# Hybrid encoder layer on one Trainium2 core: four blocks of the first FFN with one group by sevens, and the preparation, the first quarters and a block's norms in another order

## The chip, the core and the metric

One core of a Trainium2 chip runs one launch of the kernel. The time is the device time of that launch in microseconds, the median of several executions. The engines are named as the profile names them: PE is TensorE (matmuls; PEld its weight loads), DVE is VectorE, ACT is ScalarE, POOL is GpSimd and SP is SyncE, which only issues DMAs. ACT and POOL issue DMAs too.

## The reference

One layer of a streaming encoder, for 256 positions of width 2048, all in float32:

```
x = x + 0.5 * swiglu(rms_norm(x, ffn1_norm), ffn1_w_gate, ffn1_w_up, ffn1_w_down)
h = rms_norm(x, mix_norm);  u, q, k, v = split(h @ w_in)
y_ssm = s5_mixer(u, ...)                 # diagonal complex state space, 64 groups of 16 channels
y_sb  = stick_breaking_attention(rms_norm(q), rms_norm(k), v)      # 8 heads of 128
x = x + concat(rms_norm(y_ssm), rms_norm(y_sb)) @ w_out
x = x + 0.5 * swiglu(rms_norm(x, ffn2_norm), ffn2_w_gate, ffn2_w_up, ffn2_w_down)
x = x + rms_norm((p @ w_ple_proj) * sigmoid(rms_norm(x, ple_norm) @ w_ple_gate))

def swiglu(h, w_gate, w_up, w_down):
    return (silu(h @ w_gate) * (h @ w_up)) @ w_down
```

The hidden width of an FFN is 5632. The S5 mixer needs matrices that depend on the parameters alone (powers of the discretised state matrix, its products with B and C); the kernel computes them itself. This is called the preparation below.

## The kernel before, in words

**Products.** A float32 matrix product is made of three products of float32r parts. `split` (L179) casts a tile to its high part on ScalarE (`whi`, `nhi`; L182) and subtracts that from the tile on VectorE to get the low part (`wlo`, `nlo`; L185). `gemm_half` (L295) then multiplies, for two k tiles of 128 rows, high by high and low by high (L301, 8 matmuls of 512 columns for the two row blocks of 128 positions) and high by low (L308, 4 matmuls). A quarter is four k tiles of one weight matrix, 512 columns wide: one load of 1 MB on SP's queue into one of three `raw` buffers, two splits, 24 matmuls. `gemm_block` (L327) runs the four quarters of a block of 512 output columns.

**The FFN** (`ffn`, L538) runs over 11 blocks of 512 hidden columns, gate and up for each, then the down product. A block is plain, or it is a pair: `Pairs` (L357) takes [gate | up] as one matrix and one or two of its four groups of four k tiles by sevens, that is by seven products in place of eight over 2 x 2 blocks (two row blocks, two halves of k, gate and up). `prepare_left` (L367) forms the sums of the activations, four operations of 128 x 256 and a split (`shi`, `slo`); `fetch` (L390) loads both weight tiles (`dg`, `du`) and forms three sums of weights on VectorE (`t1`, `t2`, `t4`, L415) and one on a DMA that adds (`du<-du`, on GpSimd's queue, L419). `sevens` (L423) makes the products (`product`, L310: 4 matmuls of L318 and 2 of L322) into four accumulators, with additions and subtractions between them on VectorE (L431 to L439). `rest` (L462) runs the remaining groups plainly. In the first FFN blocks 0 to 6 are plain and 7 to 10 take two groups by sevens (`FIRST_PAIRS`, L30). In the second FFN block 0 takes one group and the others two; the final gate product has one group as well.

**What runs beside.** Generators stand in a list `beside`; `step` (L104), called after each half, runs each one on to its next yield. `put_off(n, f)` calls f n steps later. So the loads and transposes of norms, the squares for their means, the sums of the weights and the preparation are interleaved with the matmuls by counting steps. The instructions are then put in order for each engine at build time by a planner with its own costs; `pin` keeps an instruction in program order, and `tc.issue_after` ties instructions behind another on its engine. Each engine works through its own queue in order.

**The preparation** (`s5_prep_steps`, L865) starts after block 0 of the first FFN and goes one yield per step until `EARLY`, at which `finish(prep)` runs what is left. Its last part has four rounds `q`: eight complex products (`cmul`, L948: six VectorE operations each), copies into padded tiles on ScalarE, 16 transposes and 16 small matmuls on TensorE, and stores of the results to scratch in DRAM (`scr`), issued by ScalarE. One of them, `m3`, is placed piece by piece in a tile by 16 ScalarE copies (L1077) and stored whole.

**Around it.** `first_quarters` (L245) loads and splits the first two quarters' weights and activations in pieces; the activations' second quarter comes by ACT's queue. `turn_quarters` (L223) finishes a transpose across 128 partitions by 16 DMAs from a tile `mid`, for hidden blocks into DRAM (`hidden`) on SP's queue, and for the normed activations of some blocks on GpSimd's. `Normed.block` (L483) does this for one quarter of x, with `parted` (the split with the gain, L193 and L195) a number of steps later and `squares` after one step. `project` (L1474) makes the output projection and puts off `n2.block` for the second FFN's norm.

Of the kernel before, what the change touches and what calls it, by code (L numbers as in the profile page):

```python
# [28 lines left out]
EARLY = 6  # L29
FIRST_PAIRS = 7,()  # L30
# [7 lines left out]
def layer_kernel(ctx: ExitStack, tc: tile.TileContext, a: dict, shapes: dict, out: bass.AP):  # L38
# [84 lines left out]
    last_sevens = []  # L123

    @contextmanager
    def behind_sevens():
# [96 lines left out]
    def turn_quarters(out, mid, steps, queue=None):  # L223
# [3 lines left out]
        def g():  # L227
            for _ in range(steps):
                yield
            for i in range(4):  # L230
                for q in range(4):
                    (queue or nc.sync).dma_start(  # L232
                        out[32 * q : 32 * q + 32, :, i], mid[32 * i : 32 * i + 32, q]
                    )
# [10 lines left out]
    def first_quarters(w, xn):  # L245

        rest = com("h")
        raws = [wp.tile([P, 4, NB], F32, tag="raw", name=uid("raw"), bufs=3) for _ in range(2)]
        src = [w[i * NB : (i + 1) * NB, :NB].rearrange("(j p) n -> p j n", p=P) for i in range(2)]
        for j in range(4):  # L250
            nc.sync.dma_start(raws[0][:, j, :], src[0][:, j, :])
# [7 lines left out]
        part = halves("n")  # L259
        parts = [[wp.tile([P, 2, NB], F32R, tag=s, name=uid(s)) for s in ("whi", "wlo")] for _ in range(2)]  # L260
        for j in range(4):
            xj = rest[:, (j - 1) * T : j * T] if j else gains[:, NCOL:]
            xhi, xlo = (u[:, j, :] for u in part)
            whi, wlo = (u[:, j % 2, :] for u in parts[j // 2])
            gain = col(xn.gain, j)
            if j:
                pin(nc.scalar.activation(xhi, xj, AF.Copy, scale=gain))
            else:
                pin(nc.vector.tensor_scalar(xhi, xj, gain, None, op0=ALU.mult))
            pin(nc.scalar.copy(whi, raws[0][:, j, :]))  # L270
            pin(nc.vector.scalar_tensor_tensor(
                out=xlo, in0=xj, scalar=gain, in1=xhi.bitcast(F32), op0=ALU.mult, op1=ALU.subtract
            ))
            pin(nc.vector.tensor_tensor(out=wlo, in0=raws[0][:, j, :], in1=whi.bitcast(F32), op=ALU.subtract))
        xn.parts[0] = part
        xn.parted(1, second.rearrange("p (j s) -> p j s", j=4))
        return [(h, *parts[h]) for h in range(2)], weight_split(raws[1], 4)

    def weight_split(raw, nk, own=None):
        for h in range(nk // 2):  # L280
# [4 lines left out]
            split(hi, lo, raw[:, 2 * h : 2 * h + 2, :])  # L285
            yield h, hi, lo

# [7 lines left out]
    def gemm_half(ps, half, ts, start, stop, cols=slice(0, NB), apart=False, **kw):  # L295
# [3 lines left out]
        for j in range(2):  # L299
# [5 lines left out]
        for j in range(2):  # L305
            for t in ts:
                lh = ahi[:, 2 * h + j, t * P : (t + 1) * P]
                nc.tensor.matmul(ps[t], lhsT=lh, rhs=lo[:, j, cols], start=False, stop=stop and j == 1, **kw)  # L308

    def product(ps, a, src, start):  # L310

        (ahi, alo), hi, lo = a, *(wp.tile([P, 2, NB], F32R, tag=s, name=uid(s)) for s in ("whi", "wlo"))
        marks = split(hi, lo, src)

# [12 lines left out]
    def gemm_block(act, w, n0, nkt, first=(), but=None):  # L327

        ps = [acc(), acc()]
        for k0 in range(0, nkt, 4):  # L330
            part = act(k0 // 4)
            quarter = first[k0 // 4] if k0 // 4 < len(first) else weight_halves(w, k0, min(4, nkt - k0), n0)
            for half in list(quarter):
# [4 lines left out]
                step(but if k0 + 4 >= nkt else None)  # L338
# [18 lines left out]
    class Pairs:  # L357
# [5 lines left out]
        def __init__(self, xn, buf):  # L363
            self.xn, self.buf = xn, buf
            self.left, self.right, self.sums = [], {}, {}

        def prepare_left(self, tag="h"):  # L367
# [4 lines left out]
            pin(nc.vector.tensor_tensor(out=full, in0=part[0].bitcast(F32), in1=part[1].bitcast(F32), op=ALU.add))  # L372
# [4 lines left out]
            a11, a12, a21, a22 = (quarter(full, t, k) for t in range(2) for k in range(2))  # L377
            for o, x, y, op in (
                (a22, a21, a22, ALU.subtract), (a21, a11, a21, ALU.subtract), (a11, a22, a11, ALU.subtract),
                (a12, a12, a11, ALU.add),  # L380
# [1312 lines left out]
```

## Time and profile before

| | us |
|---|---|
| median of 3 runs | 1853.39 (1853.13 to 1853.56) |
| the profiled execution | 1853.61 |
| its span | 1851.8 |

| stage, us from the span's start | what runs |
|---|---|
| 0 to 49 | block 0 of the first FFN |
| 49 to 273 | blocks 1 to 5, with the preparation |
| 273 to 317 | block 6 |
| 317 to 482 | blocks 7 to 10, two groups by sevens |
| 482 to 730 | down product |
| 730 to 1047 | mixer, attention, output projection |
| 1047 to 1510 | second FFN, gate and up |
| 1510 to 1852 | down product, the per-layer embedding |

The edges of the stages are read from the activations and gated products of the blocks and are rough by a few us. A row of an engine's timeline gives the start, the duration, the engine, the line, the operation, the tile written and the tiles read, and a count where neighbours of one kind are merged; in brackets stands how long the engine was idle before, and what ended that. Rows of busy time by stage give, for each engine, its busy us and in brackets its number of instructions. A duration of a matmul overlaps with the next ones; its pace is read from start to start.

### The profile page before, as it was taken

The numbers are of one execution on the slowest core, as the hardware profiler recorded it, in microseconds if no ns is written. First come the engines' busy times: TensorE is split into PE (matmuls) and PEld (weight loads), VectorE is DVE, ScalarE is ACT, GpSimd is POOL, SyncE is SP. The second block draws the span as 40 slices with busy tenths as digits, with TensorE's granted clock in tenths as the row PEclk, the third lists the DMA queues.
The fourth block names the chain that finished last, engine by engine and source line by source line (L and its number), as shares of the span: only waits on it lengthen the run. The fifth ranks groups of instructions, "written<-read, shape, count | busy, mean of one in ns | idle before, by whom it ended". The sixth has DMA issues, their size and how long they took to land.

```text
span 1851.8 us, 24382 instructions
## 1 busy us (share of the span) xinstructions
PE 1841.6 (99%) x8884; PEld 1517.1 (82%) x8884; DVE 1501.2 (81%) x1984; ACT 1109.7 (60%) x1354; POOL 108.1 (6%) x174
## 2 busy tenths in 40 slices
PE   9999999999999999999999999999999999999998
PEld 7888878888888888888898788888888888888886
DVE  8895767999777997686556999999889977799865
ACT  7446665566555666455784666556566655566654
POOL 0010000000000002010012510000000000000200
PEclk9999999999999999999999999999999999999999
DMA  9787878676888758675647667878777688875843
GB/s 322 255 273 232 290 257 284 205 227 218 286 262 279 235 192 300 231 259 182 205 137 269 214 203 246 269 237 265 222 244 227 219 289 265 273 237 193 279 156 140
DMA packets 272729, 443.49 MB, mean 239 GB/s; under 512 B 18784, under 2 KB 87776, under 8 KB 272480
## 3 DMA queue, kind: packets, MB, share of 16 engines
q1 hardware_dynamic: 252448, 408.01, 65.1%
q0 software_dynamic: 7392, 18.88, 4.9%
q10 hardware_dynamic: 12768, 15.04, 2.3%
q8 instruction: 69, 1.13, 0.3%
q14 instruction: 52, 0.43, 0.1%
HBM read 393.64 MB, written 26.21 MB: 227 GB/s over the span
## 4 chain that ended last, share of the span: by engine, by line
PE 96%; DMA 2%; DVE 1%; POOL 1%; ACT 0%; issue 0%; SPq 0%; DVEq 0%; POOLq 0%
PE acc L301 47%; PE acc L308 24%; PE acc L318 12%; PE acc L322 6%; PE aux L318 2%; PE aux L322 1%; DMA h<-mid 1%; POOL h L232 1%; DVE wlo L185 0%; PE aux L1134 0%; PE acc L1413 0%; PE acc L1408 0%; PE acc L1404 0%; PE aux L1046 0%; DMA raw<-in_ffn_w_gate 0%
## 5 line engine op out<-in xcount | busy, mean ns | idle before, releaser
L182 ACT CAST whi<-raw 128x1024 fp32r<-128x1024 f32 x506 | 526.0, 1052 | 415.3 <-PE acc L301 290.5
L185 DVE TENSOR_TENSOR wlo<-raw,whi 128x1024 fp32r<-128x1024 f32 x506 | 608.7, 1223 | 201.4 <-ACT whi L182 200.5
L301 PE MATMUL acc<-whi,nhi 128*128 128x512 f32 x1424 | 558.0, 392 | 0.9 <-ACT whi L182 0.4
L301 PE MATMUL acc<-whi,nlo 128*128 128x512 f32 x1424 | 554.3, 389 | 0.0
L308 PE MATMUL acc<-wlo,nhi 128*128 128x512 f32 x1424 | 382.3, 389 | 0.4 <-DVE wlo L185 0.4
L301 PEld LDWEIGHTS acc<-whi,nhi 128*128 128x128 f32 x1424 | 267.1, 188 | 59.1 <-issue 1.6
L308 PEld LDWEIGHTS acc<-wlo,nhi 128*128 128x128 f32 x1424 | 267.2, 188 | 56.6 <-DVE wlo L185 0.8
L301 PEld LDWEIGHTS acc<-whi,nlo 128*128 128x128 f32 x1424 | 267.4, 188 | 54.6
L301 PE MATMUL acc<-whi,hhi 128*128 128x512 f32 x560 | 219.2, 391 | 0.1
L301 PE MATMUL acc<-whi,hlo 128*128 128x512 f32 x560 | 218.3, 390 | 0.0
L182 ACT CAST whi<-t 128x1024 fp32r<-128x1024 f32 x119 | 125.1, 1051 | 108.5 <-PE acc L301 62.9
L185 DVE TENSOR_TENSOR wlo<-t,whi 128x1024 fp32r<-128x1024 f32 x119 | 141.8, 1220 | 32.1 <-ACT whi L182 31.9
L308 PE MATMUL acc<-wlo,hhi 128*128 128x512 f32 x560 | 149.8, 389 | 0.3 <-DVE wlo L185 0.3
L301 PEld LDWEIGHTS acc<-whi,hhi 128*128 128x128 f32 x560 | 105.1, 188 | 24.4 <-ACT whi L182 1.1
L301 PEld LDWEIGHTS acc<-whi,hlo 128*128 128x128 f32 x560 | 105.1, 188 | 22.5
L308 PEld LDWEIGHTS acc<-wlo,hhi 128*128 128x128 f32 x560 | 105.0, 188 | 22.5 <-DVE wlo L185 0.7
L318 PE MATMUL acc<-whi,shi 128*128 128x512 f32 x240 | 95.5, 398 | 0.0
L318 PE MATMUL acc<-whi,slo 128*128 128x512 f32 x240 | 94.3, 393 | 0.0
L182 ACT CAST whi<-dg 128x1024 fp32r<-128x1024 f32 x60 | 63.0, 1051 | 37.6 <-PE acc L301 23.8
L232 POOL DMA_DIRECT2D h<-mid x96 | 51.0, 542 | 582.1 <-DVE mid L218 538.6
L185 DVE TENSOR_TENSOR wlo<-dg,whi 128x1024 fp32r<-128x1024 f32 x60 | 72.4, 1210 | 9.2 <-ACT whi L182 8.7
L322 PE MATMUL acc<-wlo,shi 128*128 128x512 f32 x240 | 75.5, 396 | 0.0
(336 smaller groups left out, 2197.5 us busy)
## 6 DMA issues: line engine op xcount, KB each, us to landing
raw<-in_ffn_w_down SPq DMA_DIRECT2D x68, 1024.0 KB, 6.5
raw<-in_ffn_w_up SPq DMA_DIRECT2D x59, 1024.0 KB, 7.8
raw<-in_ffn_w_gate SPq DMA_DIRECT2D x57, 1024.0 KB, 7.1
raw<-in_w_in SPq DMA_DIRECT2D x32, 1024.0 KB, 5.6
dg<-in_ffn_w_gate SPq DMA_DIRECT2D x29, 1024.0 KB, 7.0
du<-in_ffn_w_up SPq DMA_DIRECT2D x29, 1024.0 KB, 8.7
hf<-hidden SPq DMA_DIRECT2D x44, 512.0 KB, 5.4
raw<-in_w_out SPq DMA_DIRECT2D x16, 1024.0 KB, 5.5
```

Source lines behind the costliest of these rows:

```text
L182: copy = nc.scalar.copy(hi, src)
L185: rest = nc.vector.tensor_tensor(out=lo, in0=src, in1=hi.bitcast(F32), op=ALU.subtract)
L232: (queue or nc.sync).dma_start(out[32 * q : 32 * q + 32, :, i], mid[32 * i : 32 * i + 32, q])
L301: nc.tensor.matmul(ps[t], lhsT=u[:, 2 * h + j, t * P : (t + 1) * P], rhs=hi[:, j, cols], start=t in starts and j == 0 and u is ahi, stop=F ...
L308: nc.tensor.matmul(ps[t], lhsT=lh, rhs=lo[:, j, cols], start=False, stop=stop and j == 1, **kw)
L318: nc.tensor.matmul(ps, lhsT=l[:, j], rhs=hi[:, j], start=start and i + j == 0, stop=False, skip_group_check=True)
L322: nc.tensor.matmul(ps, lhsT=ahi[:, j], rhs=lo[:, j], start=False, stop=j == 1, skip_group_check=True)
```

## The change

- `FIRST_PAIRS` becomes 4,(4,5,6,7): blocks 4 to 7 of the first FFN take one group by sevens, 8 to 10 two. `EARLY` becomes 7.
- The preparation's rounds yield after each complex product; a round's outputs (transposes, small matmuls, stores) run as a generator of their own beside the next round's products. All stores go to GpSimd's queue, in program order. `m3` is no longer placed in a tile: zeros are written to its scratch (`cleared`), and 16 small DMAs write its pieces.
- `behind` ties the preparation, `prepare_left` and the pinned sums of weights behind the last split made; `prepare_left` becomes a generator of three steps. With `weave`, one of the two steps of a quarter comes between its two splits.
- The hidden stores of blocks 0 to 5 go to GpSimd's queue, in program order, four steps earlier.
- `first_quarters` brings the second quarter's activations by SP's queue in two halves, each ahead of its weights, and splits in the order of the halves; within the first quarter the low products of a k tile follow its high products (`gemm_half` with `apart`).
- `n2.block`: other counts of steps for the split and the squares of each of the four blocks, and block 3 begins four steps later.

```diff
-EARLY = 6
-FIRST_PAIRS = 7,()
+EARLY = 7
+FIRST_PAIRS = 4,(4,5,6,7)
...
+    def behind(splits):
         with ExitStack() as held:
-            for ins in last_sevens:
+            for ins in splits:
                 held.enter_context(tc.issue_after(ins))
             yield
...
     def first_quarters(w, xn):
-        rest = com("h")
+        rest, second = com("h"), com("h")
...
-        second = xn.laid(1)
+        for j in range(4):
+            nc.sync.dma_start(raws[0][:, j, :], src[0][:, j, :])
         for j in range(0, 4, 2):
+            nc.sync.dma_start(
+                second[:, j * T : (j + 2) * T], a["turned"][:, NCOL + (4 + j) * T : NCOL + (6 + j) * T]
+            )
             nc.sync.dma_start(raws[1][:, j : j + 2, :], src[1][:, j : j + 2, :])
...
+        for h, whi, wlo in quarters[1]:
+            sl = slice(2 * h, 2 * h + 2)
+            for low in (*activations(1, (2 * h, 2 * h + 1), x1), weights(whi, wlo, raws[1][:, sl, :])):
+                low()
+        return quarters
...
-            split(hi, lo, raw[:, 2 * h : 2 * h + 2, :])
+            last_split[:] = split(hi, lo, raw[:, 2 * h : 2 * h + 2, :])
             yield h, hi, lo
+
+    def woven(quarter, but, weave):
+        if not weave:
+            yield from list(quarter)
+            return
+        first = next(quarter)
+        step(but)
+        second = next(quarter)
+        yield first
+        yield second
...
+        for part, j in ((high, 0), (low, 0), (high, 1), (low, 1)) if apart else ((high, 0), (high, 1), (low, 0), (low, 1)):
+            part(j)
...
-                gemm_half(ps, (part, half), range(TT), k == 0, k + 2 == nkt, apart=bool(first) and k == 0)
+                gemm_half(ps, (part, half), range(TT), k == 0, k + 2 == nkt, apart=bool(first) and k < 4)
...
-                    with behind_sevens():
-                        ins = nc.vector.tensor_tensor(out=o, in0=x, in1=y, op=ALU.add)
-                    if pinned:
-                        pin(ins)
+                    with behind(last_split if pinned else last_sevens):
+                        nc.vector.tensor_tensor(out=o, in0=x, in1=y, op=ALU.add)
...
-                turn_quarters(hf.rearrange("p (t i f b) -> p t i f b", t=TT, i=4, f=n_pair), mids[pair], 8)
+                turn_quarters(
+                    hf.rearrange("p (t i f b) -> p t i f b", t=TT, i=4, f=n_pair), mids[pair], 4 if bg and f < early else 8,
+                    *((nc.gpsimd, pin) if f < early and bg else ()),
+                )
...
-                if len(pairs.left) < n_groups(f + 1):
-                    with behind_sevens():
-                        pairs.prepare_left("sg")
...
+            if f + 1 < NF and len(pairs.left) < n_groups(f + 1):
+                pairs.prepare_left("sg")
...
+        def outputs(q):
...
-                m1 = get(sub, "m1")
+                m1 = get(sub, "m1", bufs=2)
                 nc.scalar.copy(m1, ps)
-                nc.scalar.dma_start(scr[n][q], m1)
+                pin(nc.gpsimd.dma_start(scr[n][q], m1))
...
+            for r in range(4):
+                for sidx in range(SL):
+                    pin(nc.gpsimd.dma_start(
+                        m3[32 * sidx : 32 * sidx + 32, :, r, 32 * sidx :],
+                        rows[32 * r : 32 * r + 32, :, : P - 32 * sidx],
+                    ))
+                yield
+            if q + 1 < NQ:
+                pin(cleared(q + 1))
             yield
...
-            put_off(0, n2.block, n, (1, 9 if n else 6), nc.gpsimd)
+            put_off(0 if n < ND - 1 else 4, n2.block, n, ((1, 6, 3), (1, 9, 3), (1, 12, 3), (1, 6, 4))[n], nc.gpsimd)
```

More of the change, by code (lines that the diff above doesn't have):

```diff
@@ L221, in turn_blocks, with turn_quarters @@
         )
-    def turn_quarters(out, mid, steps, queue=None):
+    def turn_quarters(out, mid, steps, queue=None, held=lambda ins: ins):
         def g():
@@ L261, in first_quarters @@
-        for j in range(4):
[L262 to L274, printed above, removed]
@@ L275, in first_quarters, with activations @@
-        xn.parts[0] = part
-        xn.parted(1, second.rearrange("p (j s) -> p j s", j=4))
-        return [(h, *parts[h]) for h in range(2)], weight_split(raws[1], 4)
+        parts = [halves("n") for _ in range(2)]
+        xn.parts.update(enumerate(parts))
+        quarters = [
+            [(h, *(wp.tile([P, 2, NB], F32R, tag=s, name=uid(s)) for s in ("whi", "wlo"))) for h in range(2)]
+            for _ in range(2)
+        ]
+        def activations(i, js, src):
+            for j in js:
+                xhi, gain = parts[i][0][:, j, :], col(xn.gain, 4 * i + j)
+                if i + j:
+                    pin(nc.scalar.activation(xhi, src[j], AF.Copy, scale=gain))
+                else:
+                    pin(nc.vector.tensor_scalar(xhi, src[j], gain, None, op0=ALU.mult))
+            return [
+                lambda j=j: pin(nc.vector.scalar_tensor_tensor(
+                    out=parts[i][1][:, j, :], in0=src[j], scalar=col(xn.gain, 4 * i + j),
+                    in1=parts[i][0][:, j, :].bitcast(F32), op0=ALU.mult, op1=ALU.subtract,
+                )) for j in js
+            ]
@@ new lines, in weights @@
+        def weights(hi, lo, src):
+            pin(nc.scalar.copy(hi, src))
+            return lambda: pin(nc.vector.tensor_tensor(out=lo, in0=src, in1=hi.bitcast(F32), op=ALU.subtract))
+        x0 = [gains[:, NCOL:]] + [rest[:, j * T : (j + 1) * T] for j in range(3)]
+        x1 = [second[:, j * T : (j + 1) * T] for j in range(4)]
+        for j in range(4):
+            _, whi, wlo = quarters[0][j // 2]
+            for low in (*activations(0, [j], x0), weights(whi[:, j % 2, :], wlo[:, j % 2, :], raws[0][:, j, :])):
+                low()
@@ L304, in gemm_half, with low @@
                 )
-        for j in range(2):
+        def low(j):
             for t in ts:
@@ L371, in prepare_left @@
             full = com(tag).rearrange("p (j t) -> p j t", t=T)
[L372 removed]
+            sums = tuple(self.buf(n, i).rearrange("p (j t) -> p j t", t=T) for n in ("shi", "slo"))
             def quarter(u, t, k):
                 return u[:, 2 * k : 2 * k + 2, t * P : (t + 1) * P]
[L377 to L380, printed above, removed]
[L381 to L384 removed]
             self.left.append((
@@ L460, in sevens, with rest @@
             return [a, x], [y, z]
-        def rest(self, ps, col, groups, but=None):
+        def rest(self, ps, col, groups, but=None, weave=False):
             w, n0 = col
@@ L612, in pair @@
                 nc.scalar.activation(sg[:, t * NB : (t + 1) * NB], ps, AF.Silu, scale=xn.rs(t))
-            pairs.rest(right, (wu, f * NB), groups, prep)
+            pairs.rest(right, (wu, f * NB), groups, prep, bool(prep))
             hh = com("h")
@@ L1084, in s5_prep_steps @@
+        for _ in outs:
             yield
```

173 lines of the change are left out of this document (98 added, 75 removed).

## The prediction

> **What bounds the kernel now.** I read the page first (engines, then the chain that ended last), then the chain in order of time, then the busy time of each engine by stage, and last the stretches in which TensorE fell out of step.
>
> ```profile
> span 1851.8 us, 24382 instructions
> PE 1841.6 (99%) x8884; PEld 1517.1 (82%) x8884; DVE 1501.2 (81%) x1984; ACT 1109.7 (60%) x1354; POOL 108.1 (6%) x174
> PE 96%; DMA 2%; DVE 1%; POOL 1%; ACT 0%; issue 0%; SPq 0%; DVEq 0%; POOLq 0%
> 23.42 1.81 PE acc L301 x8
> 26.14 1.81 PE acc L301 x8
> ```
>
> TensorE carries 96% of the chain. The last two lines are one half quarter after another in block 0 of the first FFN: 8 matmuls of L301 and 4 of L308, 2.72 us from start to start, so 12 matmuls at 0.2267 us. That is the pace, and a change can win in two ways only: fewer matmuls, or fewer moments out of step.
>
> The profiled execution took 1853.61 us, 1.81 us outside its span, and lies 0.22 us above the median of 1853.39. I make the sum against 1853.61 and take 0.22 off at the end.
>
> **Term 1: the products.** A group of four k tiles as plain products costs two quarters, 48 matmuls, 4 x 2.72 = 10.88 us. By sevens it is seven products of 6. Their pace in block 7 of before, from the second matmul group of each product:
>
> ```profile
> 326.69 0.61 PE L322 MATMUL acc<-wlo,nhi 128*128 128x512 f32 x2
> 328.06 0.61 PE L322 MATMUL acc<-wlo,nhi 128*128 128x512 f32 x2
> 329.44 0.63 PE L322 MATMUL acc<-wlo,shi 128*128 128x512 f32 x2
> 330.84 0.63 PE L322 MATMUL acc<-wlo,shi 128*128 128x512 f32 x2
> ```
>
> A product with a plain left part (nhi) takes 1.37 us, one with a sum (shi) 1.40 us. Three and four of them make 9.71 us, 1.17 less than plain. Blocks 4, 5 and 6 get one such group where they had none; block 7 has one where it had two. Net two groups: -2.34 us. In matmuls it is 12 fewer, -2.72 us if all ran at 0.2267; I keep the slower pace of the sums.
>
> **Term 2: the first quarters.**
>
> ```profile
> 5.07 0.72 PE L301 MATMUL acc<-whi,nhi 128*128 128x512 f32 x2
> 17.82 0.39 PE L301 MATMUL acc<-whi,nhi 128*128 128x512 f32 x1
> 5.53 0.51 ACT L267 ACTIVATE nhi<-h,gains 128x256 fp32r<-128x256 f32 x1 [0.53 <-DMA h<-in_turned]
> 9.02 0.62 ACT L270 CAST whi<-raw 128x512 fp32r<-128x512 f32 x1 [0.36 <-DMA raw<-in_ffn_w_gate]
> 9.55 1.70 ACT L193 ACTIVATE nhi<-h,gains 128x256 fp32r<-128x256 f32 x4
> 11.16 1.98 ACT L182 CAST whi<-raw 128x1024 fp32r<-128x1024 f32 x2
> DMA packets 3320, 6.92 MB, mean 346 GB/s; under 512 B 224, under 2 KB 480, under 8 KB 3320
> ```
>
> The first real matmul starts at 5.07, the first of the third quarter at 17.82; between them lie two quarters, 48 matmuls, 10.88 us. So 12.75 - 10.88 = 1.87 us are lost. Three edits touch this. The low products of a k tile come right behind its high ones, so TensorE has two matmuls (0.45 us) to do while ScalarE makes the next tile's high part. The second quarter's activations (512 KB) leave ACT's queue and follow the first weights on SP's, so the tile that ScalarE waited for at 9.02 shares the engines with 512 KB less: at 346 GB/s, 1.5 us earlier, about 7.5. And ScalarE does two activations and one cast (0.85 + 1.0 us) before the second quarter can begin, not four and one (1.7 + 1.0). Counted on: from 5.53 three pairs of activation and cast at 0.93 us bring ScalarE to 8.3, two activations to 9.2. The first half of the second weights stands behind 262 + 524 KB, 2.3 us after 7.5, at 9.8; its cast ends at 10.8. An unbroken TensorE would come there at 5.07 + 24 x 0.2267 = 10.51. I leave 0.4 us lost: -1.5 us. Nothing is put ahead of the first weight tiles, so the bounds are 0 and -1.87.
>
> **Term 3: into the second FFN.** Same method, with each matmul counted between two rows:
>
> ```profile
> 1035.73 1.07 PE L308 MATMUL acc<-wlo,nhi 128*128 128x512 f32 x4
> 1041.89 1.07 PE L308 MATMUL acc<-wlo,nhi 128*128 128x512 f32 x4
> 1061.55 0.63 PE L322 MATMUL acc<-wlo,shi 128*128 128x512 f32 x2
> 1069.07 0.62 PE L308 MATMUL acc<-wlo,hhi 128*128 128x512 f32 x2
> 1058.99 1.71 ACT L193 ACTIVATE nhi<-h,gains 128x256 fp32r<-128x256 f32 x4
> 1063.20 1.67 DVE L195 SCALAR_TENSOR_TENSOR nlo<-h,gains,nhi 128x256 fp32r<-128x256 f32 x4
> ```
>
> 1035.73 to 1041.89 holds 24 matmuls (5.44 us): 0.72 lost. 1061.55 to 1069.07 holds 28 (6.35 us): 1.17 lost, as block 0 of the second FFN passes from its sevens to its plain rest. In front of that stand, on ScalarE and then on VectorE, the four activations and four subtractions of n2's block 2 (last two rows), ahead of the rest's casts and low parts. The change gives block 2's split 12 steps in place of 9: three steps later, out of the sevens and behind the rest's first quarter. Its squares and block 3's transposes move back too. Block 2 is then wanted one quarter (5.4 us) later, and 1.7 + 1.05 us of ScalarE fit under it; block 3's split now falls just before its quarter, with no such room. I take -1.0 of the 1.17. The 0.72 comes from VectorE, packed with prepare_left's six operations; these now stand behind the projection's splits, step by step, but their sum is the same: -0.3 of 0.72. Term 3: -1.3 us, between +1.0 (block 3's split late by most of its 1.7 us) and -1.9.
>
> **Term 4: what the sevens cost in blocks 4 to 7.**
>
> ```profile
> 93.00:137.00 44.00, 44.00 (x196) 36.45 (x195) 40.29 (x100) 20.37 (x24) 5.30 (x7) 1.00 0.82 269
> 137.00:182.00 45.00, 45.00 (x232) 36.64 (x232) 28.08 (x67) 28.54 (x51) 0.00 (x0) 1.00 0.70 227
> 182.00:228.00 46.00, 46.00 (x241) 37.52 (x241) 33.87 (x73) 32.54 (x53) 0.00 (x0) 1.00 0.89 291
> 358.00:399.00 41.00, 41.00 (x181) 33.67 (x180) 37.37 (x37) 23.85 (x26) 1.72 (x2) 1.00 0.75 237
> 182.00:228.00 46.00, 10.37 (x48) 1.00 0.89 291
> L185 DVE TENSOR_TENSOR wlo<-raw,whi x506: 1179/1220/1762, 12.2 to 1824.1; 128x1024 fp32r<-128x1024 f32 x169
> L665 DVE SCALAR_TENSOR_TENSOR h<-acc,sm,sg x14: 741/744/752, 53.3 to 326.4; 128x512 f32<-128x512 f32 x14
> L218 DVE STREAM_TRANSPOSE mid<-h x44: 669/705/708, 55.8 to 1512.0; 128x512 f32<-128x512 f32 x44
> L415 DVE TENSOR_TENSOR t<-dg,du x30: 1217/1220/1226, 306.0 to 1756.5; 128x1024 f32<-128x1024 f32 x30
> 335.41 0.70 DVE L435 TENSOR_TENSOR acc<-acc,c 128x512 f32<-128x512 f32 x1 [0.20 <-ACT c L434]
> 340.37 0.40 PE L318 MATMUL acc<-whi,slo 128*128 128x512 f32 x1
> 340.75 0.73 PE L322 MATMUL acc<-wlo,shi 128*128 128x512 f32 x2
> 341.31 0.40 PE L318 MATMUL acc<-whi,shi 128*128 128x512 f32 x1
> ```
>
> The columns are TensorE, weight loads, VectorE, ScalarE, POOL, clock, DMA share, GB/s. The first four rows are blocks 2, 3 and 4 and a block with two groups by sevens, which keeps VectorE busy for 37.37 of 41 us. The fifth is the preparation's products alone (tile cm) in block 4: 48 operations, 8 products, so 1.3 us of VectorE for one. A block with one group needs 19 splits and 3 sums at 1.22 us (26.8), four joining operations at 0.70 (2.8), and two gated products and two transposes (2 x 0.74 + 2 x 0.70 = 2.9): 32.5. By the yields, blocks 4 to 6 have ten steps of preparation each and about six products, 7.8 us: 40.3 us of the 42.3 + 0.9 that TensorE takes with the preparation's matmuls. That is no more than the two-group blocks bear. Inside the sevens (9.7 us) VectorE has 7 x 1.22 + 2.8 = 11.3 us: 1.6 too much, which the splits made ahead must hide. In block 7 of before they nearly did: 340.37 to 340.75 is 0.15 over the pace, and from there to 341.31, two matmuls on, it is 0.11 more. I take that 0.26 for each of blocks 4 to 6: +0.8 us, between 0 and 3 x 1.6 = +4.8. Block 3 takes one prepare_left, about 4 us, beside its preparation; block 2 of before had VectorE busy for 40.29 of 44 us and stayed in step: nothing.
>
> **At nothing.**
>
> ```profile
> 277.99 4.70 ACT L1077 COPY m<-aux 32x256 f32<-32x256 f32 x16 [1.69 <-DVE aux L1069]
> L232 POOL DMA_DIRECT2D h<-mid x96: 533/533/590, 703.8 to 1732.1; - x96
> L232 SPq DMA_DIRECT2D h<-mid x64: 585/595/1361, 602.1 to 1661.0; - x64
> du<-du POOLq DMA_DIRECT2D x2, 512.0 KB, 8.1
> 314.12 0.85 POOL L419 DMA_DIRECT2D du<-du  x1 [5.57 <-DVE t L415]
> ```
>
> The first row is the sixteen copies that placed m3 for one round: they leave ScalarE, 4.70 us four times. ScalarE has a third of its time free in blocks 3 and 4 (28.54 of 45, 32.54 of 46) and is not on the chain: 0. The preparation, prepare_left and the sums are now tied behind the last split on their engine; that is an order and adds no wait. The preparation's stores (23 in each of four rounds) and the hidden stores of three pairs of blocks (48) go to GpSimd's queue: 140 x 0.533 = 75 us of POOL over some 270 us; SP sheds the 48 at 0.595. By the yields, 76 of 84 steps are done when block 7 begins; the rest, mostly sixteen small stores, comes at once on POOL, under block 7. Block 8's second pair of weights goes where the preparation's tiles lay, and behind its DMA on SP's queue stand the next weights of block 7. The last 21 stores take 11.2 us of POOL from block 7's start; that DMA is issued after the sevens and a half, 9.7 + 2.7 = 12.4 us in: 0, and if the landing adds 2 us, the three raw buffers cover it.
>
> **Sum.** -2.34 - 1.5 - 1.3 + 0.8 = -4.3 us: 1849.3 against the profiled execution, 1849.1 as a median. About 0.2%, 3.7 us, is what a measurement of this kernel can tell from no change; the forecast lies just past it.
>
> **Rivals.**
>
> *VectorE falls behind in the sevens.* Term 4 at its far end, +4.8 for +0.8: 1849.1 + 4.0 = 1853.1, no change. For it: 11.3 us of work in 9.7, in blocks that carry preparation. Against it: the two-group blocks, with 14 x 1.22 + 2.8 = 19.9 in 19.4, run in step, and no preparation is issued within the sevens.
>
> *The two ends stay.* Terms 2 and 3 at 0: another wait (the weights' DMA at the start, the quarter transposes' landing in the projections) ends last. 1853.39 - 2.34 + 0.8 = 1851.9, no change.
>
> *GpSimd's queue becomes the last.* The fourth of the seven products needs du's half with its partner added, and that adding DMA now shares POOL's queue with stores kept in program order. From the sum t1 (step 8 of a block, 9.7 + 4 x 2.72 = 20.6 us in) to the split of that product in the next block lie 42.3 - 20.6 + 4.1 - 2.3 = 23.5 us. Landing takes 8.1 and issue about 0.9; at 0.533 us, 27 stores fit ahead of it, and 28 at most come in that stretch (16 hidden, 12 of the preparation). It decides from 0.52 us a store if all 28 stand ahead. At the adding DMA's own 0.85 us a store (28 x 0.85 + 9.0 = 32.8) it would be 9.3 us late in blocks 5, 6 and 7: +27.9, 1877.0. Against it: at step 8 only 4 hidden stores are issued.
> The Trainium skill (SBUF — State Buffer, section "A bandwidth-pool intuition that's wrong (but worth ruling out)") speaks against moving stores there: VectorE can lock GpSimd out of writing descriptors, 620 ns becoming 3100; by that figure 28 stores would take an estimated 87 us, two whole blocks. This trace has 96 such stores at 533 to 590 ns beside a VectorE 81% busy and does not agree.
>
> **Chances.** Forecast 0.66, of which 0.56 lies past the 3.7 us and 0.10 short of them; VectorE behind 0.18; the two ends stay 0.09; GpSimd's queue 0.07. Faster 0.56, within 0.2% 0.10 + 0.18 + 0.09 = 0.37, slower 0.07. Range: below, all bounds at once, -2.34 - 1.87 - 1.9 + 0: 1847.3; above, 1853.5 takes in the first two rivals and leaves the last out.
>
> **What would show it.** In the profile after: blocks 4 to 6 about 1.2 us shorter each, block 7 1.2 longer; the third quarter's first matmul near 16.4; from 1035 to 1070 less than 0.6 us lost. Wrong it is if the sevens of blocks 4 to 6 show waits on L185 over 0.3 us, if TensorE or ScalarE waits for du, or if the start still waits on ACT or a DMA at the second quarter.

## The result: 1869.3 us, slower

The kernel after took 1869.32 us (median of 4 runs, 1868.06 to 1870.13), the kernel before beside it 1853.26 (4 runs, 1852.20 to 1853.56): a ratio of 1.0086, 95% interval 1.0073 to 1.0099. It is 16 us slower, where the forecast was 1849.1 and the range ended at 1853.5. The profiled execution took 1869.86 us, with a span of 1868.1.

The page of the kernel after, the lines that answer to those of before: TensorE's row, GpSimd's row, the chain, TensorE's low products, and GpSimd's share in 40 slices.

```profile
span 1868.1 us, 24460 instructions
PE 1844.5 (99%) x8872; PEld 1518.0 (81%) x8872; DVE 1521.4 (81%) x2008; ACT 1103.2 (59%) x1305; POOL 188.6 (10%) x316
POOL 0022342400000002000013420000000000000200
PE 94%; DMA 2%; issue 2%; POOL 1%; DVE 1%; ACT 0%; ACTq 0%; DVEq 0%
L340 PE MATMUL acc<-wlo,nhi 128*128 128x512 f32 x1392 | 376.2, 391 | 12.9 <-DVE wlo L185 12.9
```

TensorE has its 12 matmuls less (8872 for 8884), but the low products idled 12.9 us for VectorE's low parts, and "issue" has come into the chain with 2% (some 37 us). GpSimd is busy for less than half of any slice, so its busy share does not show what held its queue. To place the loss I took the distance from the start of each 512-column matmul to the start of the next matmul and counted what is over the pace of 0.2267: 26.1 us lost in all before, 44.2 after. The 18 us more, less 2.7 for the 12 matmuls, are nearly the whole 16. Outside 225 to 375 us the two kernels lose the same within 1 us. Inside there are two large gaps, and each is one row of TensorE's timeline (by the count just given they are 4.38 and 8.46 us):

```profile
247.90 2.07 PE L340 MATMUL acc<-wlo,nhi 128*128 128x512 f32 x4 [4.22 <-DVE wlo L185]
350.84 1.65 PE L340 MATMUL acc<-wlo,nhi 128*128 128x512 f32 x3 [8.29 <-DVE wlo L185]
```

The wait on L185 is where the last release came from, not yet the cause. VectorE's own timeline in the kernel after says what VectorE was doing:

```profile
240.16 0.69 DVE L491 TENSOR_TENSOR acc<-c,acc 128x512 f32<-128x512 f32 x1
245.43 1.30 DVE L218 STREAM_TRANSPOSE mid<-h 128x512 f32<-128x512 f32 x2 [4.58 <-DMA scr_m<-blocks]
246.66 2.32 DVE L185 TENSOR_TENSOR wlo<-raw,whi 128x1024 fp32r<-128x1024 f32 x2
348.37 1.30 DVE L218 STREAM_TRANSPOSE mid<-h 128x512 f32<-128x512 f32 x2 [9.05 <-DMA hidden<-mid]
```

It stood still, 4.58 and 9.05 us, in front of the transposes into `mid`, with the splits that TensorE needed queued behind them. There is one `mid`; it can be written again only when the hidden stores of the pair of blocks before have read it. (The row at 245.43 names `scr_m`, a store in the same queue that landed last; by the code it is the hidden stores among them that the transposes need.) Those stores are now on GpSimd's queue, in order. GpSimd's timeline in the kernel after, at the second stall:

```profile
311.91 0.77 POOL L1086 DMA_DIRECT2D scr_cpr<-cb  x1 [7.89 <-issue]
318.15 0.77 POOL L1086 DMA_DIRECT2D scr_cpr<-cb  x1 [5.47 <-issue]
323.65 0.75 POOL L1086 DMA_DIRECT2D scr_cpi<-cb  x1 [4.73 <-issue]
330.07 0.76 POOL L1086 DMA_DIRECT2D scr_cpi<-cb  x1 [5.67 <-issue]
330.82 3.75 POOL L232 DMA_DIRECT2D hidden<-mid  x7
```

The four stores of one round of the preparation (`cpr` and `cpi`, 512 rows of 512 B each, a row being one contiguous run) come 5.5 to 6.4 us apart, although each occupies GpSimd for only 0.77 us. In front of each it waited for nothing that the profile shows ("issue"). Seven hidden stores follow at once when the fourth is through.

What a stall costs beyond its own length is seen in three stretches of the second one. Columns: length; busy time and instructions of TensorE, weight loads, VectorE, ScalarE, POOL; granted clock; DMA share; GB/s.

```profile
331.00:342.10 11.10, 11.10 (x49) 9.02 (x49) 8.25 (x10) 8.30 (x10) 8.42 (x17) 1.00 0.91 288
342.10:350.70 8.60, 0.44 (x2) 0.02 (x1) 2.33 (x3) 0.00 (x0) 7.34 (x15) 0.70 0.53 173
350.70:354.00 3.30, 3.16 (x8) 2.49 (x9) 3.30 (x4) 1.04 (x1) 0.43 (x1) 0.50 0.33 56
```

After the gap the clock is 0.50 and TensorE does 8 matmuls in 3.30 us, where its pace is 14. The stretch has a price of 19 us in all: 21.6 us are lost from 225 to 375 in the kernel after, 2.5 in the same stretch of the first experiment, in which the stalls are gone.

A smaller part of it, 1.55 us at 236.80, has another victim of the same queue, the adding DMA of `du`. It was issued at 227.34, behind the four stores of another round, and these are the rows of ScalarE and of GpSimd when it landed:

```profile
232.74 1.05 ACT L182 CAST whi<-du 128x1024 fp32r<-128x1024 f32 x1 [5.33 <-PE acc L358]
232.87 0.51 POOL L1109 DMA_DIRECT2D scr_m<-blocks  x1 [0.78 <-DMA du<-du]
```

The first row names TensorE. But in e1, below, the same cast starts 4 us earlier (228.76), and here it starts just as `du` lands, as the second row shows.

### The profile page after: what moved, and what is told of

Same layout as the page of the kernel before. It is cut to its first block, busy times and chain, and to the rows that moved or that the text cites. A ratio compares the mean times of both kernels' runs of the same rounds, so it can differ in the third digit from the quotient of the medians.

```text
span 1868.1 us, 24460 instructions
## 1 busy us (share of the span) xinstructions
PE 1844.5 (99%) x8872; PEld 1518.0 (81%) x8872; DVE 1521.4 (81%) x2008; ACT 1103.2 (59%) x1305; POOL 188.6 (10%) x316
## 3 DMA queue, kind: packets, MB, share of 16 engines
q8 instruction: 69, 1.13, 0.2%
## 4 chain that ended last, share of the span: by engine, by line
PE 94%; DMA 2%; issue 2%; POOL 1%; DVE 1%; ACT 0%; ACTq 0%; DVEq 0%
PE acc L332 46%; PE acc L340 23%; PE acc L354 12%; PE acc L358 6%; PE aux L354 2%; PE aux L358 1%; DMA hidden<-mid 1%; DMA raw<-in_ffn_w_gate 0%; PE aux L1207 0%; PE aux L1079 0%; PE acc L1486 0%; PE acc L1481 0%; PE acc L1477 0%; POOL hidden L232 0%; DMA h<-in_turned 0%
## 5 line engine op out<-in xcount | busy, mean ns | idle before, releaser
L182 ACT CAST whi<-raw 128x1024 fp32r<-128x1024 f32 x496 | 517.2, 1052 | 432.4 <-PE acc L332 292.6
L185 DVE TENSOR_TENSOR wlo<-raw,whi 128x1024 fp32r<-128x1024 f32 x496 | 597.0, 1223 | 171.1 <-ACT whi L182 170.2
L332 PE MATMUL acc<-whi,nhi 128*128 128x512 f32 x1392 | 546.6, 393 | 0.4 <-ACT whi L284 0.2
L332 PE MATMUL acc<-whi,nlo 128*128 128x512 f32 x1392 | 542.0, 390 | 0.0
L340 PE MATMUL acc<-wlo,nhi 128*128 128x512 f32 x1392 | 376.2, 391 | 12.9 <-DVE wlo L185 12.9
L340 PEld LDWEIGHTS acc<-wlo,nhi 128*128 128x128 f32 x1392 | 262.0, 188 | 69.1 <-DVE wlo L185 14.2
L182 ACT CAST whi<-t 128x1024 fp32r<-128x1024 f32 x125 | 131.4, 1051 | 114.8 <-PE acc L332 70.3
L185 DVE TENSOR_TENSOR wlo<-t,whi 128x1024 fp32r<-128x1024 f32 x125 | 149.3, 1220 | 39.4 <-ACT whi L182 39.2
L340 PE MATMUL acc<-wlo,hhi 128*128 128x512 f32 x560 | 149.6, 389 | 0.0
L340 PEld LDWEIGHTS acc<-wlo,hhi 128*128 128x128 f32 x560 | 105.1, 188 | 21.9
L354 PE MATMUL acc<-whi,shi 128*128 128x512 f32 x256 | 102.0, 398 | 1.4 <-DVE acc L487 1.4
L354 PE MATMUL acc<-whi,slo 128*128 128x512 f32 x256 | 100.6, 393 | 0.0
L185 DVE TENSOR_TENSOR wlo<-dg,whi 128x1024 fp32r<-128x1024 f32 x64 | 77.3, 1212 | 14.4 <-ACT whi L182 14.0
```

The lines of the kernel that those rows point to most:

```text
L182: copy = nc.scalar.copy(hi, src)
L185: rest = nc.vector.tensor_tensor(out=lo, in0=src, in1=hi.bitcast(F32), op=ALU.subtract)
L332: nc.tensor.matmul(ps[t], lhsT=u[:, 2 * h + j, t * P : (t + 1) * P], rhs=hi[:, j, cols], start=t in starts and j == 0 and u is ahi, stop=F ...
L354: nc.tensor.matmul(ps, lhsT=l[:, j], rhs=hi[:, j], start=start and i + j == 0, stop=False, skip_group_check=True)
```

## The experiments

**Theory one:** each `cpr` or `cpi` store holds GpSimd's queue for some 5 us, the hidden stores are pinned behind them, `mid` is read late, VectorE's transposes wait, the splits behind them are late, TensorE idles and its clock falls. **Rivals:** R1, the 64 small stores of `m3` do it by their number; R2, the pinned order does it, whatever the stores; R3, VectorE is overfull with sevens and preparation in blocks 4 to 7.

The first four were run beside 25 runs of the kernel before (median 1852.84). Where a later run is compared with e1, a second figure takes each against the kernel before of its own session.

**e1_cp_act.** One part undone:

```
-                    pin(nc.gpsimd.dma_start(
+                    nc.scalar.dma_start(
                         scr[n][q][:, b * 512 : (b + 1) * 512].rearrange("p (r c) -> p r c", r=4),
                         cb[i][b].rearrange("p (r c) -> p r c", r=4)[:, :, 32:],
-                    ))
+                    )
```

> The kernel after, with one part undone: the preparation's cpr and cpi stores (16 in all, four per round, each of 512 rows of 512 B) are issued on ScalarE's queue as in the kernel before, instead of pinned on GpSimd's. All else stays, the hidden stores and the 64 small m3 stores on GpSimd's queue included. Theory one (these stores hold GpSimd's queue 3 to 8 us each; the first FFN's hidden stores are pinned behind them, so the one mid buffer is read late, VectorE's next transposes wait, and the weight splits behind those starve TensorE): the two stalls of the kernel after, 4.38 us at 243.30 and 8.46 us at 342.16, go, with the matmuls at half clock behind them, and the time falls from 1869.3 by about 17 us to 1850 to 1853; no hidden store waits over 1 us for its issue. Rival R1 (it is the number of small m3 stores): the stalls stay, 1865 to 1870. Rival R2 (the pinned order itself, whatever the stores): 1865 to 1870. Rival R3 (VectorE is overfull in blocks 4 to 7 with groups by sevens and the preparation beside them): 1862 to 1870.

Measured: 1849.36 us (1848.39 to 1850.66, 10 runs), ratio to before 0.9979 (0.9970 to 0.9989). That is 20 us less than the kernel after, through 16 stores, and 0.6 below the range expected. No hidden store waits over 0.4 us for its issue. The same two stretches, in the kernel after and then in this one:

```profile
225.00:260.00 35.00, 29.33 (x135) 22.62 (x134) 25.19 (x46) 16.62 (x20) 18.39 (x33) 0.90 0.79 246
325.00:356.00 31.00, 22.70 (x90) 18.08 (x89) 18.52 (x22) 12.01 (x13) 17.13 (x32) 0.83 0.73 239
```

```profile
225.00:260.00 35.00, 35.00 (x188) 28.17 (x187) 32.34 (x68) 22.99 (x30) 9.20 (x18) 1.00 0.85 281
325.00:356.00 31.00, 31.00 (x138) 25.56 (x137) 30.05 (x33) 17.27 (x18) 1.81 (x2) 1.00 0.90 269
```

TensorE is busy throughout, and VectorE does more in the same time (32.34 us for 25.19) because it stands still no longer. R3 and R1 fall: the sevens, the preparation and all 64 `m3` stores are unchanged here. So does R2 in its plain form, since the pinned order of the rest is kept.

**e2_hidden_sp.** The other end of the chain undone: the `(nc.gpsimd, pin)` of the hidden stores is taken out, so that they go on SyncE's queue.

> The kernel after, with another part undone: the hidden stores of the blocks beside the preparation go back to SyncE's queue, in eight steps as in the kernel before; all the preparation's stores stay in order on GpSimd's queue. Theory one: the cpr and cpi stores still wait 3 to 8 us each for their issue, but nothing that VectorE waits for stands behind them, so both stalls go: 1850 to 1855, the upper part if SyncE's queue holds weight loads back behind the hidden stores. R1 and R2, as ways in which the hidden stores get late, say the same here (1850 to 1855). R3 (VectorE overfull): the stalls stay, 1862 to 1870.

Measured: 1854.80 us (1852.30 to 1858.07, 10 runs), ratio 1.0010 (1.0001 to 1.0020). Both stalls go, as the theory says; 5.4 us stay against e1. The `cpr` and `cpi` stores still wait (72 us for issue in all), and `du` behind them is late: twice ScalarE stood 4.5 us in front of a cast of `du`, with a gap of 1.01 us on TensorE behind each (at 237.57 and 284.84). e6 below bears on the rest.

**e3_cp_rows.** Same bytes, same queue, a quarter of the rows:

```
-                    pin(nc.gpsimd.dma_start(
-                        scr[n][q][:, b * 512 : (b + 1) * 512].rearrange("p (r c) -> p r c", r=4),
-                        cb[i][b].rearrange("p (r c) -> p r c", r=4)[:, :, 32:],
-                    ))
+                    pin(nc.gpsimd.dma_start(scr[n][q][:, b * 512 : (b + 1) * 512], cb[i][b][:, 32:544]))
```

> The kernel after, with each cpr and cpi store as 128 rows of 2 KB in place of 512 rows of 512 B: the same bytes, the same queue, the same place in its order. (It stores columns 32 to 543 of each buffer, not the right ones, so the S5 stage computes with wrong values.) If the number of rows is what holds GpSimd's queue, each of these stores waits under 1 us for its issue, as the 128-row stores of other arrays do, and the time falls to 1850 to 1854. If it is the bytes or the order (256 KB must drain before the next one is issued), the waits of 3 to 8 us stay and so does the time, 1865 to 1870. R1 and R3 say 1862 to 1870 too.

Measured: 1849.20 us (1848.24 to 1850.71, 10 runs), ratio 0.9979 (0.9970 to 0.9988). It is the number of rows and not the bytes. The view of the stores' line in the kernel after: duration of each (least, median, most, in ns), what their engine waited for in front of them (us, times), and how long from issue to landing.

```profile
L1086 POOL DMA_DIRECT2D scr_cpr<-cb x8: 762/772/782, 160.8 to 318.2; - x8
L1086 POOL DMA_DIRECT2D scr_cpi<-cb x8: 750/756/759, 175.0 to 330.1; - x8
  issue: 71.1, 14
DMA to landing us min/median/max: 2.8/5.1/8.5
```

The same view of this kernel:

```profile
L1086 POOL DMA_DIRECT2D scr_cpr<-cb x8: 547/553/889, 157.3 to 294.9; - x8
L1086 POOL DMA_DIRECT2D scr_cpi<-cb x8: 539/539/880, 158.3 to 302.0; - x8
  issue: 7.6, 3
DMA to landing us min/median/max: 6.1/6.9/11.2
```

The transfer is no faster with 128 rows (6.9 us to landing for 5.1); what has gone is the wait in front of the stores, 71.1 us in 14 waits to 7.6 in 3. Those three are still 1.6 to 3.5 us long, where under 1 us was expected.

**e4_m3_four.** 48 of the 64 small stores left out (`for sidx in range(1)` for `range(SL)`).

> The kernel after, with 48 of the 64 small m3 stores left out: of each round's 16 pieces only four are stored, 4 on GpSimd's queue in place of 16. (The S5 stage lacks the other blocks of m3, so part of the computation is left out.) Theory one: the cpr and cpi stores, which stand ahead of the m3 pieces, hold the queue as before; 48 issues of about 0.55 us less (26 us over four rounds) lets the hidden stores through somewhat earlier, so that at most a third of the stalls goes: 1862 to 1869. R1 (the number of small stores is the cause): the stalls go, 1850 to 1854. R3: 1865 to 1870.

Measured: 1861.97 us (1859.47 to 1862.52, 4 runs), ratio 1.0045 (1.0030 to 1.0060). The first stall nearly went (2.2 us lost from 225 to 250, for 7.8), the second stayed (8.4 lost from 325 to 350, for 8.7). That is 7.3 us of 20, a little over my third: the `m3` stores stand among the hidden ones and delay them by their number, but where four `cpr` and `cpi` stores stand ahead, leaving them out helps nothing.

**e5_ring_2048.** No store moved; more room for GpSimd's descriptors. To make place for it the squares are written as bf16, and one scratch tile shares another's space (not shown below). The next four were run beside 33 runs of before (median 1853.06).

```
...
-    nc = _bacc.Bacc("TRN2", target_bir_lowering=False, num_devices=1, dynamic_dma_scratch_size=1024)
+    nc = _bacc.Bacc("TRN2", target_bir_lowering=False, num_devices=1, dynamic_dma_scratch_size=2048)
```

> The kernel after, all its stores where they are, with the program's setting for the memory that holds GpSimd's DMA descriptors (dynamic_dma_scratch_size) doubled from 1024 to 2048. To make place for it the squares, of which only the sums are used, are written as bf16, and one 32-column scratch tile shares another's space. Theory 1a (a store of 512 rows fills the room for descriptors, so that the next issue waits until it has drained): with twice the room the waits for issue of the cpr and cpi stores fall from 71 us in all to under 35, the stalls of 4.4 and 8.5 us shrink or go, and the time is 1850 to 1858. Theory 1b (GpSimd needs that time to work out 512 descriptors, or a fixed pause follows such a store): the waits stay at 60 to 75 us and the time at 1865 to 1870.

Measured: 1849.45 us (1848.41 to 1850.94, 10 runs), ratio 0.9980 (0.9971 to 0.9989). The stores' line here has the numbers 1088, two lines further down:

```profile
L1088 POOL DMA_DIRECT2D scr_cpr<-cb x8: 765/775/981, 157.3 to 295.8; - x8
L1088 POOL DMA_DIRECT2D scr_cpi<-cb x8: 752/754/762, 160.7 to 304.7; - x8
  issue: 24.7, 8
```

Theory 1a holds and 1b falls: GpSimd works on each store as long as before (0.77 us), so the 5 us were a wait for room. With twice the room the first two or three stores of a round pass at once, and the waits are 8 for 14, 24.7 us. The two edits that make place have little part in the time: in e11 below the whole of this edit, on top of e1, changes 0.5 us.

**e6_both.** The edits of e1 and e2 together.

> Both moves at once: the cpr and cpi stores on ScalarE's queue and the hidden stores of the early blocks back on SyncE's, in eight steps; only the m1, m3 and zero stores stay on GpSimd's queue. It tells what kept the kernel with the hidden stores on SyncE's queue alone at 1854.8 where the one with the cpr and cpi stores on ScalarE's gave 1849.4. If it is the hidden stores themselves (32 issues of some 0.5 us per pair of blocks ahead of the weight loads on SyncE's queue), this kernel gives 1853 to 1855. If it is the du sums, held behind the cpr and cpi stores on GpSimd's queue, it gives 1849 to 1850.5.

Measured: 1853.68 us (1851.49 to 1855.64, 11 runs), ratio 1.0004 (0.9996 to 1.0013). So by the medians, of the 5.4 us between e2 and e1, 4.3 are the hidden stores on SyncE's queue, and 1.1 the du sums behind the `cpr` and `cpi` stores. The split is rough: the runs of e2 and of this kernel spread over 4 to 6 us, and the two gaps behind `du` in e2's trace are 2.0 us by themselves. In this kernel the largest wait of ScalarE between 100 and 150 us is for weights (us in all, times, the longest):

```profile
ACT whi L182 <- DMA raw<-in_ffn_w_up: 15.4, 4, 4.7
```

Two gaps of 1.46 and 0.77 us on TensorE follow there, at 119.96 and 127.03. In e1 the same row has 8.7 us in 3 waits, and TensorE lost nothing between 100 and 150. SyncE issues 16 hidden stores for this pair of blocks (16, not the 32 of the expectation) between 100.4 and 114 us, with the loads of the next weights among them. In before the same stores stood there and 0.1 us was lost in that stretch; why they cost more after the change was not followed further.

**e7_no_sevens.** e1 with `EARLY = 6` and `FIRST_PAIRS = 7,()`.

> The kernel with the cpr and cpi stores on ScalarE's queue (1849.4), with the groups by sevens as in the kernel before: two in block 7 and none in blocks 4 to 6 (FIRST_PAIRS 7 and EARLY 6, with which the hidden stores of blocks 6 and 7 are on SyncE's queue). The prediction's term of products (two more groups by sevens, 2.34 us saved) and its term of their cost (0.8 us) say 1849.4 + 2.34 - 0.8 = 1850.9; if the sevens cost nothing beside the preparation, 1851.7; rival R3 (the sevens beside the preparation overfill VectorE and lose what they save): 1847.5 to 1849.6.

Measured: 1852.38 us (1851.69 to 1854.13, 11 runs), ratio 0.9996 (0.9987 to 1.0005). The sevens are worth 3.0 us against e1 (2.8 by each session's before), more than forecast (1.5), and R3 is refuted a second time. EARLY moves no hidden store to another queue: 48 of them are on GpSimd's in this kernel as in e1. It does move the end of the preparation, which this run does not part from the sevens.

**e8_n2_steps.** e1 with `put_off(0, n2.block, n, (1, 9 if n else 6), nc.gpsimd)` as before.

> The kernel with the cpr and cpi stores on ScalarE's queue (1849.4), with the step counts of the second FFN's normalised blocks as in the kernel before, all else as after. The prediction's third term (1.3 us, two stalls at the start of the second FFN) says 1850.7, with about 1.9 us lost by TensorE between 1025 and 1075 in place of 0.25. If those stalls came from the preparation's order or another part of the change, the time stays at 1849.0 to 1849.8.

Measured: 1850.71 us (1849.52 to 1852.71, 11 runs), ratio 0.9987 (0.9978 to 0.9996). The third term is 1.35 us by the medians (1.1 by each session's before). The runs of the two kernels overlap, so the trace has to show that it is there. From TensorE's timeline of this kernel, then of e1: the last product with a sum of the second FFN's block 0, and the low products of the half quarter behind the first plain one, 28 matmuls (6.35 us) later.

```profile
1058.92 0.63 PE L358 MATMUL acc<-wlo,shi 128*128 128x512 f32 x2
1066.40 0.84 PE L340 MATMUL acc<-wlo,hhi 128*128 128x512 f32 x3
```

```profile
1057.27 0.63 PE L358 MATMUL acc<-wlo,shi 128*128 128x512 f32 x2
1063.66 1.07 PE L340 MATMUL acc<-wlo,hhi 128*128 128x512 f32 x4
```

7.48 us in the one, 1.13 lost, as the 1.17 of before; 6.39 in the other, 0.04 lost.

**e9_first.** e1 with `first_quarters`, `gemm_half` and the `apart` condition of the kernel before. The last four were run beside 28 runs of before (median 1853.07).

> The kernel with the cpr and cpi stores on ScalarE's queue (1849.4), with the preparation of the first quarters, the order of the first loads and the order of block 0's products as in the kernel before. The prediction's second term (1.5 us of start-up stalls saved) says 1850.9, with about 1.9 us lost by TensorE in the first 25 us. If the start depends on when the first transfers land, which differs from run to run (0.9 to 2.0 us were lost there in profiles of kernels with one and the same start), the term is smaller: 1849.4 to 1850.3.

Measured: 1850.06 us (1849.90 to 1850.63, 11 runs), ratio 0.9983 (0.9975 to 0.9992). By the medians the second term is 0.7 us (0.5 by each session's before), half of the 1.5 forecast or less. The intervals of this kernel and of e1 (0.9970 to 0.9989) overlap for the most part, so that even this much is not clear of noise.

**e10_cp_256.** As e3, with two rows of 1 KB a partition (`r=2` and `[:, :, 32:288]`).

> The kernel after, with each cpr and cpi store as 256 rows of 1 KB: the same bytes, queue and place, half the rows. (It stores columns 32 to 287 of each half buffer, not the right ones, so the S5 stage computes with wrong values.) If each row takes a place in GpSimd's room for descriptors and 1024 holds one store of 512 rows, two of 256 fit: the waits for issue fall from 71 us to 15 to 40, as with the room doubled (24.7), and the time is 1849 to 1854. If only rows of 2 KB pass freely (a limit of size, not of number), the waits stay over 55 us and the time at 1862 to 1870.

Measured: 1849.25 us (1848.38 to 1849.77, 10 runs), ratio 0.9978 (0.9969 to 0.9987).

```profile
L1086 POOL DMA_DIRECT2D scr_cpr<-cb x8: 727/731/947, 157.5 to 302.8; - x8
L1086 POOL DMA_DIRECT2D scr_cpi<-cb x8: 712/715/732, 162.2 to 306.2; - x8
  issue: 25.9, 8
```

Half the rows in the old room wait as all rows in twice the room: 25.9 us in 8 waits, 24.7 in 8. What counts is rows against room, and the room of 1024 behaves as if it held about one store of 512 rows.
The Trainium skill (DMA: Bandwidth & Descriptors, section "SWDGE vs HWDGE vs iDMA") has GpSimd write its descriptors into rings in a part of SBUF set aside for them, and another section of the page ("Why a DMA increments its semaphore by 16 and not by 1") has one descriptor move one contiguous run: by that, a store of 512 runs takes four times the places of one of 128. These runs agree.

**e11_act_ring.** Both cures, e1's edit on e5.

> Both cures at once: the cpr and cpi stores on ScalarE's queue and GpSimd's room for descriptors doubled (with the bf16 squares and the shared scratch tile). As each alone gave 1849.4 and no GpSimd store there waits for its issue, the theory says no gain on top: 1848.9 to 1849.9. A gain of over 0.5 us would mean that the room still holds something back (the m3 pieces or the du sums).

Measured: 1848.86 us (1848.50 to 1849.53, 10 runs), ratio 0.9977 (0.9967 to 0.9986). No gain on top that the runs can tell from e1, as expected. Both, and e5 alone, beat the kernel before and the kernel after.

**e12_hidden_first.** The hidden stores' first four steps of delay taken out (`mids[pair], 0 if bg and f < early else 8`).

> The kernel after, with the early blocks' hidden stores begun at once behind the transposes instead of four steps later; queue, pins and all other stores as they are. In the theory what counts is how many cpr and cpi stores stand ahead of them in GpSimd's queue (one at the first pair that stalls, four, some 24 us, at the next): four steps earlier lets part of them pass, so that the stalls of 4.4 and 8.5 us shrink by a half or more, 1852 to 1862. If the stalls come from VectorE's own load in these blocks (R3), the time stays at 1865 to 1870.

Measured: 1858.23 us (1854.37 to 1861.15, 6 runs), ratio 1.0025 (1.0013 to 1.0037). The transposes wait no longer, and another passenger of the same queue is late, the adding DMA of `du`. From the waits of this kernel between 310 and 350 us (us in all, times, the longest):

```profile
POOL scr_cpi L1086 <- issue: 11.5, 2, 6.0
POOL scr_cpr L1086 <- issue: 6.7, 1, 6.7
ACT whi L182 <- DMA du<-du: 8.4, 1, 8.4
PE acc L354 <- ACT whi L182: 2.8, 1, 2.8
```

Its order is right for one consumer and wrong for the next; as long as the queue stands still for 5 us a store, someone behind it pays.

## Why the prediction was wrong

**The step that failed is "At nothing".** I priced the stores moved to GpSimd's queue at "140 x 0.533 = 75 us of POOL over some 270 us", all hidden. The row behind the 0.533 was of `h<-mid` stores, small ones from 32 partitions, and I carried it to stores of every shape. For 124 of the 140 it nearly held (71.0 us busy, 0.57 each). For the 16 of `cpr` and `cpi`, 512 rows each, the queue was held 0.77 us of work and 71.1 / 16 = 4.4 us of wait: 83 us for 16 stores, more than the 75 that I gave to all.

**The second half of that step:** I asked what each moved store costs its engine and who waits for `du`, but not who waits for the hidden stores themselves. The single `mid` ties them to VectorE, in front of splits that TensorE needs; that tie is in the code and stood in none of my terms.

**The third rival** named the right queue and the right order of size (1877.0 for 1869.3), with a chance of 0.07. It put the price on the number of stores (28 at 0.85) and on `du`. In the kernel after the price lay on the 16 with many rows, and at the two stalls `mid` ended last. `du` cost 1.55 us there, as shown above, some 1 to 2 us in e2, and came last in e12; so the sign "if TensorE or ScalarE waits for du" did appear. "At step 8 only 4 hidden stores are issued" spoke against it in my text: true, and no argument, since what stood ahead of them was not counted by time.
The lock of GpSimd by VectorE that this rival cites from the Trainium skill (SBUF — State Buffer, section "A bandwidth-pool intuition that's wrong (but worth ruling out)"; 620 to 3100 ns) finds no support here either: the small stores took 0.57 us in the mean beside a VectorE 81% busy, and e3 and e5 removed the waits with VectorE as busy as before.

**With that one step put right the sum comes out:** 1849.1 forecast, 1849.36 measured in e1. That they agree to 0.3 us is partly luck. In e1's own session the kernel before took 1852.84, so that the gain is 3.5 us where 4.3 was forecast, and two terms were off in opposite directions. The terms, each against a run that undoes it:

- *Products and the sevens' cost* (terms 1 and 4): -2.34 and +0.8 forecast, 2.8 to 3.0 us saved (e7). The trace agrees that nothing was paid. The gated products end a block, and where they waited for TensorE they mark its time. From VectorE's timeline of before, then of e1, the ends of blocks 6, 7 and 10:

```profile
325.76 1.41 DVE L665 SCALAR_TENSOR_TENSOR h<-acc,sm,sg 128x512 f32<-128x512 f32 x2 [1.09 <-PE acc L308]
367.21 1.41 DVE L617 SCALAR_TENSOR_TENSOR h<-acc,sm,sg 128x512 f32<-128x512 f32 x2 [1.09 <-PE acc L308]
490.73 1.41 DVE L617 SCALAR_TENSOR_TENSOR h<-acc,sm,sg 128x512 f32<-128x512 f32 x2 [1.09 <-PE acc L308]
```

```profile
321.25 1.41 DVE L675 SCALAR_TENSOR_TENSOR h<-acc,sm,sg 128x512 f32<-128x512 f32 x2 [1.09 <-PE acc L340]
363.63 1.41 DVE L675 SCALAR_TENSOR_TENSOR h<-acc,sm,sg 128x512 f32<-128x512 f32 x2 [1.09 <-PE acc L340]
487.15 1.41 DVE L675 SCALAR_TENSOR_TENSOR h<-acc,sm,sg 128x512 f32<-128x512 f32 x2 [1.09 <-PE acc L340]
```

  From the third quarter's first matmul (17.82 before, 16.68 in e1) to the end of block 10 are 472.91 us before and 470.47 in e1: 2.44 less, the 2.34 of the working and no cost. Block 7 is 0.93 longer, 1.2 forecast. (By these rows block 6 of before ends near 325, some 8 us later than the table of stages has it.) Blocks 4 to 6 cannot be compared one by one, since the preparation is spread over them in another way; in e1 they take 45.90 us each, not the 43.2 of the working, so VectorE had 2.7 us more room in each. No idle time of the low products (L340) shows in e1's page. VectorE behind (0.18) is refuted; in the kernel after it only looked so, because VectorE was made to wait.
- *First quarters* (term 2): -1.5 forecast, -0.5 to -0.7 measured (e9), not clear of noise. The third quarter's first matmul came at 16.98 in the profile after and 16.68 in e1, where I said 16.4. The start differs from execution to execution: the twelve profiles with the new order (all but e9's) lose 0.9 to 2.0 us in the first 25 us, 1.3 in the mean, where I counted on 0.4. I had worked from one landing of the first transfers as if it were fixed.
- *Into the second FFN* (term 3): -1.3 forecast, -1.1 to -1.35 measured (e8), of which the rows above show 1.09 in one place.
- By each session's before the three add to 4.4 us, and e1 is 3.5 below before in its own. Single runs lie 1 us apart, and undoings need not add; what the other 0.9 is stays open.
- *The two ends stay* is refuted by e8 for the second FFN. For the first quarters it stays open.

Of the signs named for being wrong, "waits on L185 over 0.3 us" did appear, but at plain low products and for the reason above, not for the sevens' load.

## What to carry to other kernels

When a transfer moves to another queue, price it by its own shape (rows, not only bytes), list everything queued behind it, and follow each of those to the buffer it frees and the engine that waits for that buffer. If a queue is held by "issue", try the cheap cures before reordering: fewer and longer rows, more room for descriptors, or another queue each gave back the whole 20 us here, while reordering gave 11. A wait on a slow-looking engine is read on that engine's own timeline first: VectorE's low parts were late because VectorE stood in front of a store.

## What the runs showed of the hardware

A store of many rows on GpSimd's queue can wait 3 to 9 us for its issue while GpSimd stands idle, and what is behind it in the queue waits with it; behind the fourth store of a round the seven hidden stores went out at once. The wait is 4.4 us in the mean for 512 rows of 512 B at a room of 1024, 1.5 at twice the room, 1.6 at half the rows, 0.5 at a quarter. On ScalarE's queue the same 512-row stores let TensorE run on unbroken (e1).

After an idle of 8.46 us TensorE ran at a granted clock of 0.50: some 12 matmuls at 0.427 us start to start in place of 0.227, 2.4 us on top of the gap.
The Trainium skill (TensorE: Matmul & The Clock Gate, section "What's actually happening") gives half clock after an idle window of about 3.4 us and again the full one after as long a busy time. The 8.46 us gap agrees, and so does the one of 4.38 at 243.30; the full pace came back 5.1 and 5.6 us after work had begun again. A gap of 3.0 us, shorter than that window, was followed by a low clock too: in e12 work began again at 331.57, and from 333 to 336.5 the granted clock was 0.54. Gaps of about 1.5 us (the kernel after at 236.80, e6 at 119.96) were followed by one slower matmul and then the full pace.
